# Output products of a chunked recurrence grouped by shape, and low-rank remainder products over 128 rows

## Chip, cores and metric

One core of a Trainium2 chip runs the whole forward pass in one launch. The metric is device time in microseconds (us) of an execution; smaller is better. Times before are of three runs. Clock shares say which part of full speed TensorE was granted: 1.00 is 2.4 GHz, 0.50 is 1.2 GHz.

## What is computed

A two-layer backbone over 256 latent tokens and 256 context tokens of width 1024. Each layer is a half-step SwiGLU, a token mixer, and another half-step SwiGLU. The mixer of the first layer is RWKV-7 time mixing in two directions (12 heads of 64) beside a Fourier mixing; that of the second is a gated convolution beside pooling. The change touches only the RWKV-7 part. Cut to what matters:

```python
g = jax.nn.sigmoid(gd) @ g_up
for d in range(2):
    w = jnp.exp(-DECAY_SCALE * jax.nn.sigmoid(w0[d] + jnp.tanh(wd) @ w_up[d]))   # decay, rank 64
    a = jax.nn.sigmoid(a0[d] + ad @ a_up[d])                                     # rate, rank 64
    kd = k * (1 + (a - 1) * k_a)

def step(S, inp):
    rt, wt, kt, vt, kkt, bt = inp
    sk = jnp.einsum('bhij,bhj->bhi', S, kkt)
    S = S * wt[:, :, None, :] - sk[..., None] * bt[:, :, None, :] + vt[..., None] * kt[:, :, None, :]
    return S, jnp.einsum('bhij,bhj->bhi', S, rt)

S_c, yc = wkv_scan(S0, context...)       # context first
_, yl = wkv_scan(S_c, latent...)         # then the latent tokens, whose outputs are kept
```

## The kernel before

Channels lie on partitions, tokens along the free dimension. Weights stream from HBM one 128-column tile at a time (512 KB, four buffers `wraw`) and are split into two parts, so that most products are three matmuls (`mm3`, lines 195 to 197).

The recurrence runs in chunks of 64 tokens. The 12 heads are 6 pairs; three groups of two pairs go one after the other through `chain` (line 704), each with four streams x: two pairs of heads times two directions. A chunk step does, for all four x and both heads hd: products of masked scores and state with the values (line 782, result `RH` copied by ScalarE), products with the inverse `F` (line 791, result negated into `UV` by ScalarE and VectorE), the update of the state (line 802, added into the next `XV` by VectorE, line 809), and `prep` of the next chunk (transposes 730 and 763, masked products 741 or 744, VectorE's `AG`, `RR` and `rs`, lines 748 to 759). Steps 0 to 3 are context; steps 4 to 7 are latent and also make outputs, lines 813 to 830. That is four output blocks in each of three groups, twelve in all.

An output block makes 8 sums (4 x, 2 heads), each of two products into the same PSUM columns: line 821 has `UV` against `RR`, over 128 rows; line 823 has `Xs` against `r` (`ar` for one head, `rs` for the other), over rows 0 to 63 alone. In the code they stand in turn:

```python
mm(p3[o:o + CW, x, :], lhsT=UV[:, x, hd, :], rhs=rv(S["RR"][:, hd, x, :]),
   start=True, stop=False, tile_position=(0, o), skip_group_check=True)
mm(p3[o:o + CW, x, :], lhsT=Xs[lo, x, hd, :], rhs=rv(r),
   start=False, stop=True, tile_position=(0, o), skip_group_check=True)
```

`RR`, `rs` and `Xs` have one buffer each: VectorE may write the next `RR` (line 757) and `rs` (759), and GpSimd the next `Xs` (774), only when the block has read the old ones. Each float32 product is two instruction pairs (weight load and matmul) in the trace.

Products of two ranks of 64 feed the decay and the rate. In `features` (line 541) lines 574 and 576 run over 128 rows, with the upper part of the input twice on the rows and both parts of the weight; lines 575 and 577 multiply the remainder of the input (`wa_l`, rows 0 to 63 for the decay and 64 to 127 for the rate) by the upper part of the weight, over 64 rows. There are 6 pairs of heads times 2 directions, so 24 remainder products of 512 columns. `decay_in` (line 521) makes the inputs once.

Around this, a scheduler sets the order of each engine's queue from the order of emission: while `chain` runs, `features` and `inverse` of the next group (`inverse`, line 632, is a substitution of 30 steps on VectorE) and the second layer's modulation (`ada_wide`, line 248, products of 512 columns with loads on SyncE's queue) are woven in; beside the last group stand the output projection (`project_most`, line 894) and the Fourier mixing. Each engine works its queue in order.

Of the kernel before, what the change touches and what calls it, by code (L numbers as in the profile page):

```python
# [7 lines left out]
F32 = mybir.dt.float32  # L8
F32R = mybir.dt.float32r
# [38 lines left out]
def dft():  # L48
    """[bd(cos64) | bd(sin64)] / 128, then cos256 and -sin256 by tiles of rows."""
# [13 lines left out]
def pool_counts():  # L63
    """1 / tokens of the centred windows, by the widths of the four groups."""
    t = np.arange(T)
    z = np.zeros((P, 2, T), np.float32)
    for g, w in enumerate((2, 4, 8, 16)):
        n = np.minimum(t + w - 1 - w // 2, T - 1) - np.maximum(t - w // 2, 0) + 1
        z[g % 2 * CW:g % 2 * CW + CW, g // 2, :] = 1.0 / n
    return z  # L70
# [9 lines left out]
def lay_out(a):  # L80
    """Arrays of the launch: inputs re-laid so that every load is contiguous per partition."""
# [52 lines left out]
class Net:  # L134
# [76 lines left out]
    def ada_first(self, b, r, ab):  # L211
        """Shift and scale of channel tile b of the first norm, for both streams, into columns b of ab."""
# [20 lines left out]
    def ada_rows(self, pool, vecs):  # L233
        """silu(c) along the free dimension of every partition."""
# [13 lines left out]
    def ada_wide(self, b, pool):  # L248
        """Columns 512 b .. of the second layer's modulation, in pieces of four loads."""
# [23 lines left out]
    def ada_job(self, blk, vecs):  # L273
        """Columns blk and blk + 1 of the first layer's modulation, as sums along the free dimension."""
# [13 lines left out]
    def modcol(self, l, v, m, scale=None, g=None):  # L288
        """Columns [P, KT] of modulation m; optionally scaled, or (1 + m) * g."""
# [15 lines left out]
    def stat(self, acc, hk, v, k):  # L305
        """Squares of channel tile k of stream v, added up over the tiles but the last."""
# [33 lines left out]
    def rstd_of(self, s, m, dim, eps):  # L340
        """(sum / dim + eps)^-1/2 of m blocks of tokens, a column each, to every partition."""
# [21 lines left out]
    def modulate_tile(self, k, h, vs, r, ab, yh, yl, hp):  # L363
        """y = rmsnorm(h) * a + b of channel tile k, as two float32r parts (or whole, without yl); ab[v] = (a, b) of
        stream v; r has the rates of the streams vs."""
# [14 lines left out]
    def update(self, h, k, ps, gate, acc, last=True, vs=None):  # L380
        """h += gate * ps for channel tile k of the streams vs."""
# [9 lines left out]
    def ffn(self, w, h, yh, yl, gate, acc, hp, jobs, pre, rate=None):  # L391
        """The input is normalised and shifted already; or, with rate, it is h * a with b as a column more,
        and the products get the tokens' rates of the norm."""
# [3 lines left out]
        # the first products follow the norm channel tile by channel tile  # L397
# [52 lines left out]
    def down(self, w, h, gate, acc, parts, last, jobs):  # L450
# [13 lines left out]
        # the last channel tiles stream by stream: the norm of the one during the products of the other  # L464
# [44 lines left out]
    def shift(self, m, ps, z):  # L509
        """token_shift of channel tile m from ps into z, streams side by side."""  # L510
# [10 lines left out]
    def decay_in(self, z, pool):  # L521
        """Inputs of the decay and rate projections: their upper parts in both halves of the rows, and the rest."""
        nc = self.nc
        nc.scalar.activation(z[0:CW], z[0:CW], AF.Tanh)
        w, a, l = (pool.tile([P, 2 * T], F32R, name=n) for n in ("wa_w", "wa_a", "wa_l"))
        for t, own, other in ((w, slice(0, CW), slice(CW, P)), (a, slice(CW, P), slice(0, CW))):
# [3 lines left out]
        return w, a, l  # L530
# [10 lines left out]
    def features(self, G, j, wa, kz, vz, rz):  # L541
# [9 lines left out]
        # kk: normalised per head  # L551
# [17 lines left out]
        for d in range(2):  # L569
# [5 lines left out]
            nc.tensor.matmul(pw, lhsT=uw[0:CW, d, :], rhs=wa[2][0:CW], start=False, stop=True)  # L575
            nc.tensor.matmul(pa, lhsT=ua[:, d, :], rhs=wa[1], start=True, stop=False)
            nc.tensor.matmul(pa, lhsT=ua[CW:P, d, :], rhs=wa[2][CW:P], start=False, stop=True)
# [5 lines left out]
            # log decay of a token is -DECAY / 2 * (1 + th); prefix sums per chunk  # L583
# [776 lines left out]
```

## Time and profile before

| what | us |
|---|---|
| median of 3 runs | 1640.65 |
| lowest and highest run | 1637.95, 1649.41 |
| span of the profiled execution | 1651.6 |
| TensorE matmul busy in it | 1555.6 (94%) |
| VectorE busy | 1082.6 (66%) |
| ScalarE busy | 677.3 (41%) |
| GpSimd busy | 204.9 (12%) |

The profiled execution has no time of its own beside its span. The span, from its first to its last instruction, is 10.95 us above the median of the runs, so differences worked out from the trace are taken off both. A busy TensorE is not one at its peak: ends of matmuls are modelled, and a waiting matmul counts as busy, so spacing is read from starts.

### The profile page before, as it was taken

Reading aid. Unit: us, or ns where it says so; the run is one execution under the profiler, and the core shown is the slowest. Engines: PE = TensorE matmul, PEld = TensorE weight load, DVE = VectorE, ACT = ScalarE, POOL = GpSimd, SP = SyncE. Lnnn points to the kernel's source line nnn. Section 1 sums busy time; section 2 is a strip of 40 time slices with the busy share of each in tenths; the row PEclk is TensorE's granted clock in tenths of the full one; section 3 lists DMA queues with packets and bytes.
Section 4 is the critical chain, followed back from the end, with each engine's and each line's share of the span. In section 5 each row is a group of like instructions: output and inputs, shape, how many; then the busy total and the mean of one; then the engine's idle time right before and its main releaser. Section 6 shows DMA issues by size and latency. Waiting matters only on the chain.

```text
span 1651.6 us, 29927 instructions
## 1 busy us (share of the span) xinstructions
PE 1555.6 (94%) x12102; PEld 1319.8 (80%) x12102; DVE 1082.6 (66%) x1994; ACT 677.3 (41%) x1101; POOL 204.9 (12%) x291
## 2 busy tenths in 40 slices
PE   5999999999989899899999899999999996899997
PEld 3788888888867655555587699999999985799997
DVE  4899954335689686466462577656776479767754
ACT  4431222223553542441441455444454355445442
POOL 0000100000040430330210100000000056300000
PEclk9999999999989789789995899999999997799999
DMA  9667943223222124444530355565556532435562
GB/s 370 230 242 257 346 136 103 95 84 123 77 65 96 56 93 151 158 170 148 191 104 14 116 180 186 175 187 179 181 182 176 167 102 89 141 130 185 181 177 95
DMA packets 68810, 253.40 MB, mean 153 GB/s; under 512 B 8032, under 2 KB 10864, under 8 KB 63936
## 3 DMA queue, kind: packets, MB, share of 16 engines
q1 hardware_dynamic: 64080, 219.46, 40.2%
q0 software_dynamic: 4592, 32.03, 5.4%
q8 instruction: 95, 1.56, 0.4%
q14 instruction: 43, 0.35, 0.1%
HBM read 249.36 MB, written 2.10 MB: 152 GB/s over the span
## 4 chain that ended last, share of the span: by engine, by line
PE 81%; DVE 13%; ACT 3%; issue 2%; POOL 1%; DMA 1%; SPq 0%; POOLq 0%; DVEq 0%; ACTq 0%
PE gu L195 13%; PE gu L196 13%; PE gu L197 13%; PE down L197 7%; PE down L195 7%; PE down L196 7%; PE ada L260 3%; PE mx L823 2%; PE mx L821 2%; DVE wlo L191 2%; DVE ocv L1022 1%; DVE oo L1022 1%; PE gu L1049 1%; PE pg L744 1%; PE down L802 1%
## 5 line engine op out<-in xcount | busy, mean ns | idle before, releaser
L190 ACT CAST whi<-wraw 128x1024 fp32r<-128x1024 f32 (+1 forms) x298 | 305.1, 1028 | 524.5 <-PE gu L196 224.0
L191 DVE TENSOR_TENSOR wlo<-wraw,whi 128x1024 fp32r<-128x1024 f32 (+1 forms) x298 | 356.6, 1199 | 154.0 <-ACT whi L190 146.4
L195 PE MATMUL gu<-yh,whi 128*128 128x258 f32 (+1 forms) x1408 | 438.4, 312 | 6.4 <-ACT yh L375 4.5
L196 PE MATMUL gu<-yl,whi 128*128 128x258 f32 (+1 forms) x1408 | 437.6, 311 | 0.0
L197 PE MATMUL gu<-yh,wlo 128*128 128x258 f32 (+1 forms) x1408 | 436.5, 310 | 0.2 <-DVE wlo L191 0.2
L195 PEld LDWEIGHTS gu<-yh,whi 128*128 128x128 f32 x1408 | 265.8, 189 | 24.2 <-ACT yh L375 5.7
L197 PEld LDWEIGHTS gu<-yh,wlo 128*128 128x128 f32 x1408 | 267.4, 190 | 15.2 <-DVE wlo L191 1.1
L196 PEld LDWEIGHTS gu<-yl,whi 128*128 128x128 f32 x1408 | 267.2, 190 | 14.8 <-DVE yl L377 0.9
L196 PE MATMUL down<-hl,whi 128*128 128x256 f32 (+1 forms) x704 | 217.3, 309 | 0.0
L195 PE MATMUL down<-hh,whi 128*128 128x256 f32 (+1 forms) x704 | 217.3, 309 | 0.0
L197 PE MATMUL down<-hh,wlo 128*128 128x256 f32 (+1 forms) x704 | 217.3, 309 | 0.0
L195 PEld LDWEIGHTS down<-hh,whi 128*128 128x128 f32 x704 | 134.4, 191 | 7.4
L197 PEld LDWEIGHTS down<-hh,wlo 128*128 128x128 f32 x704 | 134.4, 191 | 7.4
L196 PEld LDWEIGHTS down<-hl,whi 128*128 128x128 f32 x704 | 134.4, 191 | 7.3
L350 POOL TENSOR_TENSOR rs<-ms,mhalf 128x2 f32<-128x2 f32 (+1 forms) x9 | 10.9, 1209 | 822.8 <-DVE ms L347 822.8
L281 DVE SCALAR_TENSOR_TENSOR adaj<-adaw,cb 128x1024 f32<-128x1024 f32 x80 | 97.8, 1223 | 4.0 <-DMA adaw<-in_adat_dram 2.8
L260 PE MATMUL ada<-wraw,ccs 128*32 128x512 f32 x288 | 75.9, 669 | 1.0 <-DVE mod L269 1.0
L384 DVE SCALAR_TENSOR_TENSOR hlat<-down,mc,hlat 128x256 f32<-128x256 f32 x46 | 22.2, 483 | 62.9 <-PE down L197 62.9
L438 DVE COPY wb<-gu 128x1 f32<-128x1 f32 x132 | 20.3, 154 | 46.4 <-PE gu L197 46.4
L360 ACT CAST hh<-hd 128x256 fp32r<-128x256 f32 (+1 forms) x88 | 40.5, 461 | 23.9 <-DVE hd L433 13.1
L964 PE MATMUL gu<-yo,wraw 128*128 128x256 f32 x192 | 45.4, 396 | 1.9 <-ACT yo L375 1.9
L1006 POOL TENSOR_TENSOR opart<-opart,opr 128x256 f32<-128x256 f32 x54 | 45.2, 837 | 5.0 <-ACT opr L1004 1.2
(339 smaller groups left out, 2419.1 us busy)
## 6 DMA issues: line engine op xcount, KB each, us to landing
wraw<-in_gu_dram SPq DMA_DIRECT2D x176, 512.0 KB, 3.3
wraw<-in_ada_dram SPq DMA_DIRECT2D x72, 512.0 KB, 4.2
adaw<-in_adat_dram POOLq DMA_DIRECT2D x28, 1024.0 KB, 5.7
wraw<-in_down_dram SPq DMA_DIRECT2D x64, 448.0 KB, 3.3
wraw<-in_down_dram SPq DMA_DIRECT2D x32, 512.0 KB, 3.5
wraw<-in_win_dram SPq DMA_DIRECT2D x22, 512.0 KB, 3.5
wraw<-in_owin_dram SPq DMA_DIRECT2D x14, 512.0 KB, 3.6
ada<-in_ada_dram SPq DMA_DIRECT2D x4, 1024.0 KB, 16.8
```

The source lines that it names most:

```text
L190: nc.scalar.copy(hi[:, :k, :], raw[:, :k, :])
L191: (eng or nc.vector).tensor_tensor(out=lo[:, :k, :], in0=raw[:, :k, :], in1=hi[:, :k, :].bitcast(F32), op=ALU.subtract)
L195: mm(ps, lhsT=wh, rhs=xh, start=start, stop=False, **k)
L196: mm(ps, lhsT=wh, rhs=xl, start=False, stop=False, **k)
L197: mm(ps, lhsT=wl, rhs=xh, start=False, stop=stop, **k)
L260: nc.tensor.matmul(ps[32 * g:32 * g + 32, :], lhsT=self.cs[:, k, :], rhs=w[:, i, :], start=k < 4, stop=k >= 4, tile_position=(0, 32 * g), ...
L281: nc.vector.scalar_tensor_tensor(out=junk, in0=w[:, i, :], scalar=1.0, in1=self.cb[v], op0=ALU.mult, op1=ALU.mult, accum_out=self.mod[0, v ...
L360: self.nc.scalar.copy(hi, x)
L821: mm(p3[o:o + CW, x, :], lhsT=UV[:, x, hd, :], rhs=rv(S["RR"][:, hd, x, :]), start=True, stop=False, tile_position=(0, o), skip_group_chec ...
L823: mm(p3[o:o + CW, x, :], lhsT=Xs[lo, x, hd, :], rhs=rv(r), start=False, stop=True, tile_position=(0, o), skip_group_check=True)
L964: nc.tensor.matmul(ps[:, :n], lhsT=w[:, k, :], rhs=y[:, k, :], start=k == 0, stop=k == KT - 1)
L1006: nc.gpsimd.tensor_tensor(out=part, in0=prev, in1=pr, op=ALU.add)
```

## The change

In the output block, the eight products over 128 rows are issued first for all x and heads, and the eight over 64 rows after them. The start mark, which stood on the first product of every sum, stands on those of x = 0 alone. The remainder of the low-rank input gets a tile of 128 rows for the decay and another for the rate; GpSimd clears the other 64 rows of each with zeros once, and the remainder products run over 128 rows against the whole weight tile. Lines of the changed kernel are 2 higher from line 531 on, and 6 higher behind the output block.

```diff
     def decay_in(self, z, pool):
         nc.scalar.activation(z[0:CW], z[0:CW], AF.Tanh)
-        w, a, l = (pool.tile([P, 2 * T], F32R, name=n) for n in ("wa_w", "wa_a", "wa_l"))
-        for t, own, other in ((w, slice(0, CW), slice(CW, P)), (a, slice(CW, P), slice(0, CW))):
+        w, a, lw, la = (pool.tile([P, 2 * T], F32R, name=n) for n in ("wa_w", "wa_a", "wa_lw", "wa_la"))
+        for t, l, own, other in ((w, lw, slice(0, CW), slice(CW, P)), (a, la, slice(CW, P), slice(0, CW))):
+            nc.gpsimd.memset(l[other].bitcast(F32), 0.0)
             nc.scalar.copy(t[own], z[own])
             nc.scalar.copy(t[other], z[own])
             nc.vector.tensor_tensor(out=l[own], in0=z[own], in1=t[own].bitcast(F32), op=ALU.subtract)
-        return w, a, l
+        return w, a, lw, la
...
             nc.tensor.matmul(pw, lhsT=uw[:, d, :], rhs=wa[0], start=True, stop=False)
-            nc.tensor.matmul(pw, lhsT=uw[0:CW, d, :], rhs=wa[2][0:CW], start=False, stop=True)
+            nc.tensor.matmul(pw, lhsT=uw[:, d, :], rhs=wa[2], start=False, stop=True)
             nc.tensor.matmul(pa, lhsT=ua[:, d, :], rhs=wa[1], start=True, stop=False)
-            nc.tensor.matmul(pa, lhsT=ua[CW:P, d, :], rhs=wa[2][CW:P], start=False, stop=True)
+            nc.tensor.matmul(pa, lhsT=ua[:, d, :], rhs=wa[3], start=False, stop=True)
...
                 p3 = ps[:, :T].rearrange("p (x i) -> p x i", x=4)
+                rv = lambda x, t: t[:, ::-1] if x % 2 else t
+
                 for x in range(4):
-                    rv = (lambda t: t[:, ::-1]) if x % 2 else (lambda t: t)
+                    for hd in range(2):
+                        o = CW * hd
+                        mm(p3[o:o + CW, x, :], lhsT=UV[:, x, hd, :], rhs=rv(x, S["RR"][:, hd, x, :]),
+                           start=x == 0, stop=False, tile_position=(0, o), skip_group_check=True)
+                for x in range(4):
                     for hd in range(2):
                         o = CW * hd
                         r = S["rs"][lo, x, :] if hd else G["ar"][lo, x, c, 1, :]
-                        mm(p3[o:o + CW, x, :], lhsT=UV[:, x, hd, :], rhs=rv(S["RR"][:, hd, x, :]),
-                           start=True, stop=False, tile_position=(0, o), skip_group_check=True)
-                        mm(p3[o:o + CW, x, :], lhsT=Xs[lo, x, hd, :], rhs=rv(r),
+                        mm(p3[o:o + CW, x, :], lhsT=Xs[lo, x, hd, :], rhs=rv(x, r),
                            start=False, stop=True, tile_position=(0, o), skip_group_check=True)
```

The scheduler moves more than these lines: TensorE's queue differs from the first low-rank product on, in shape only up to the first output block, and in order from there to the end of the recurrence; behind it the queues of all engines read as before.

TensorE's queue at the last two output blocks of the third group, before (`mx` is the bank of the block; 782 and 791 are the next step's products with scores and with the inverse):

```order
L821 MATMUL mx_8236<-RR_8150,UV_8122 64x64
L823 MATMUL mx_8236<-ar_5967,Xs_8184 64x64
L821 MATMUL mx_8236<-RR_8150,UV_8122 64x64
L823 MATMUL mx_8236<-rs_8152,Xs_8184 64x64
L782 MATMUL down_8259<-XV_8121,AG_8217 64x64 x8
L791 MATMUL down_8270<-RH_8268,A_5969 64x64 x8
L821 MATMUL mx_8281<-RR_8230,UV_8123 64x64
L823 MATMUL mx_8281<-ar_5967,Xs_8257 64x64
```

The same place now (784 and 793 are the lines 782 and 791 of before):

```order
L829 MATMUL mx_8239<-ar_5970,Xs_8187 64x64
L829 MATMUL mx_8239<-rs_8155,Xs_8187 64x64
L784 MATMUL down_8262<-XV_8124,AG_8220 64x64 x8
L793 MATMUL down_8273<-RH_8271,A_5972 64x64 x8
L823 MATMUL mx_8284<-RR_8233,UV_8126 64x64 x8
L829 MATMUL mx_8284<-ar_5970,Xs_8260 64x64
L829 MATMUL mx_8284<-rs_8235,Xs_8260 64x64
```

The products of 128 rows stand together as x8, those of 64 rows behind them; what stands ahead of and behind the block is the same.

VectorE's queue at the last step of the third group, before (`XV` is the next step's state, in two halves by head; `rs` can be written only when the block ahead has read it):

```order
L809 TENSOR_TENSOR XV_8121<-down_8208,Xs_8184 64x4x64 x2
L748 TENSOR_TENSOR AG_8217<-pg_8218,cst 64x512
L757 TENSOR_TENSOR RR_8230<-pg_8218,cst 128x512
L759 COPY rs_8232<-ar_5967 64x256
L830 TENSOR_TENSOR yy_7406<-mx_8236,yy_7406 128x64 x2
```

And now:

```order
L811 TENSOR_TENSOR XV_8124<-down_8211,Xs_8187 64x4x64
L750 TENSOR_TENSOR AG_8220<-pg_8221,cst 64x512
L759 TENSOR_TENSOR RR_8233<-pg_8221,cst 128x512
L761 COPY rs_8235<-ar_5970 64x256
L811 TENSOR_TENSOR XV_8124<-down_8211,Xs_8187 64x4x64
L836 TENSOR_TENSOR yy_7409<-mx_8239,yy_7409 128x64 x2
```

The second half of `XV` moved behind the writes of `RR` and `rs`.

## Rows read from the trace of the kernel before

**Rows 1.** page, chain that ended last: by engine, by line
```profile
PE 81%; DVE 13%; ACT 3%; issue 2%; POOL 1%; DMA 1%; SPq 0%; POOLq 0%; DVEq 0%; ACTq 0%
PE gu L195 13%; PE gu L196 13%; PE gu L197 13%; PE down L197 7%; PE down L195 7%; PE down L196 7%; PE ada L260 3%; PE mx L823 2%; PE mx L821 2%; DVE wlo L191 2%; DVE ocv L1022 1%; DVE oo L1022 1%; PE gu L1049 1%; PE pg L744 1%; PE down L802 1%
```

**Rows 2.** chain by line, shares of 611:662, 720:800 and 869:914 us
```profile
by line: PE ada L260 22.5%; PE mx L823 16.6%; PE mx L821 16.3%; PE down L782 5.8%; DVE A L671 3.9%; DVE Dt L676 3.6%; PE ada L268 3.6%; PE down L791 3.6%; PE pg L744 3.3%; PE pg L741 3.2%; PE down L802 2.9%; PE mx L730 2.3%; ACT XV L732 2.3
...
by line: PE ada L260 22.4%; PE mx L823 10.3%; PE mx L821 9.9%; PE pg L744 7.2%; PE down L802 5.4%; PE ada L268 4.5%; PE misc L648 4.2%; PE down L782 4.0%; PE down L791 3.7%; ACT A L674 2.6%; PE mx L763 2.4%; ACT R L689 2.3%; ACT adas L265 2
...
by line: PE mx L821 27.1%; PE mx L823 26.8%; PE pg L744 14.1%; PE down L791 7.2%; PE down L782 7.0%; PE down L802 6.4%; PE mx L763 2.3%; PE mx L730 2.3%; PE misc L841 1.8%; ACT BK L765 1.3%; ACT UV L793 0.9%; ACT RH L785 0.8%; DVE yy L830 0
```

**Rows 3.** timeline, output block at full clock: start us, us, engine, line
```profile
633.57 0.33 PE L821 MATMUL mx<-RR,UV 128*64 128x64 f32 x2
...
633.83 0.33 PE L823 MATMUL mx<-ar,Xs 64*64 64x64 f32 x2
...
634.08 0.33 PE L821 MATMUL mx<-RR,UV 128*64 128x64 f32 x2
```

**Rows 4.** timeline, grouped run and output block at half clock
```profile
889.72 1.12 PE L782 MATMUL down<-XV,AG 128*64 128x64 f32 x16
...
890.77 0.79 PE L744 MATMUL pg<-ar,bk 64*128 64x128 f32 x2
...
897.01 0.47 PE L821 MATMUL mx<-RR,UV 128*64 128x64 f32 x2
...
903.46 1.12 PE L782 MATMUL down<-XV,AG 128*64 128x64 f32 x16
```

**Rows 5.** timeline, grouped runs at full clock, each with its follower
```profile
619.94 0.68 PE L802 MATMUL down<-UV,BK 128*64 128x64 f32 x14
620.54 0.94 PE L744 MATMUL pg<-ar,bk 64*128 64x128 f32 x12
...
641.59 0.68 PE L741 MATMUL pg<-ac,bk 64*64 64x64 f32 x16
...
642.20 1.04 PE L260 MATMUL ada<-wraw,ccs 128*32 128x512 f32 x2
```

**Rows 6.** stretches: length, busy us (instructions), clock, DMA share, GB/s
```profile
611.00:662.00 51.00, 50.12 (x476) 29.71 (x476) 34.30 (x91) 12.78 (x31) 4.82 (x9) 0.93 0.41 138
720.00:800.00 80.00, 74.69 (x978) 45.98 (x976) 49.44 (x126) 23.34 (x50) 12.19 (x18) 0.91 0.49 173
869.00:914.00 45.00, 42.87 (x303) 32.13 (x302) 11.95 (x26) 6.09 (x19) 3.16 (x3) 0.54 0.03 10
```

**Rows 7.** waits in 600:660 us: total us, times, longest
```profile
DVE RR L757 <- PE mx L821: 5.8, 3, 2.0
...
DVE yy L830 <- PE mx L823: 4.7, 1, 4.7
```

**Rows 8.** timeline of VectorE about a late output block
```profile
890.15 0.98 DVE L759 COPY rs<-ar 64x256 f32<-64x256 f32 x1
...
896.03 0.85 DVE L809 TENSOR_TENSOR XV<-down,Xs 64x256 f32<-64x256 f32 x2 [2.54 <-PE down L802]
```

**Rows 9.** timeline, 512-column and low-rank products; chain by line, 430:500
```profile
454.34 0.39 PE L196 MATMUL pg<-yl,whi 128*128 128x512 f32 x1
454.57 0.39 PE L197 MATMUL pg<-yh,wlo 128*128 128x512 f32 x1
...
685.20 0.47 PE L574 MATMUL misc<-wa_w,uw 128*128 128x512 f32 x1
...
686.88 1.91 PE L260 MATMUL ada<-wraw,ccs 128*32 128x512 f32 x12
...
by line: DVE wlo L191 11.3%; issue 9.9%; POOL inv L560 5.8%; PE pg L195 4.5%; PE pg L197 3.5%; DVE z L518 3.4%; DVE z L517 3.3%; PE misc L575 3.3%; DVE ff L589 3.3%; PE misc L574 3.3%; PE pg L196 3.2%; PE misc L629 3.1%; PE mx L197 3.0%; PE
```

**Rows 10.** timeline of GpSimd at the low-rank inputs
```profile
436.54 0.10 POOL L514 MEMSET zp<- 128x4 f32 x1 [24.05 <-DVE f L517]
```

**Rows 11.** page, DMA issues: count, KB each, median us to landing
```profile
wraw<-in_ada_dram SPq DMA_DIRECT2D x72, 512.0 KB, 4.2
```

## Prediction

> **What bounds the kernel now.** I read the chain that ended last first, since it says which engine's time is the kernel's. TensorE holds 81% of it and VectorE 13% [rows 1]; most of TensorE's part is feed-forward products, which the change leaves alone. But lines 821 and 823, a few hundred small products, stand there with about 2% each. Next I asked the chain by stretch, to see where. The twelve output blocks lie in 611 to 662 us (four, group 1), 720 to 800 us (four, group 2) and 869 to 914 us (four, group 3), and there the two lines hold 32.9%, 20.2% and 53.9% of the chain [rows 2]. That is 0.329 x 51 = 16.8 us, 0.202 x 80 = 16.2 us and 0.539 x 45 = 24.3 us, in all 57.3 us: the blocks are on the path from end to end, since TensorE works its queue in order and other engines wait behind it.
>
> Third, the timeline within a block. A row of two instructions is one product. At full clock a product starts 0.26 us after the one ahead of it, whichever of the two shapes it has [rows 3], so sixteen take 4.1 us; at half clock a block goes from 897.01 to 903.46, 6.45 us [rows 4]. The same amount of work in one shape costs far less: fourteen instructions of line 802, in the shape of line 821 (128 rows to 64 columns), are followed after 0.60 us, and sixteen of line 741, in the shape of 823 (64 rows), after 0.61 us, their followers in yet another shape [rows 5]. At half clock sixteen of line 782 take 1.05 us [rows 4]. So it isn't the products that cost, it is each turn from one row count to the other.
>
> **The change, part by part.** *Output blocks.* 32 instructions per block stay; the turns inside fall from fifteen to one. Two runs of sixteen at about 0.65 us (0.60 for fourteen, 0.61 for sixteen) make 1.3 us at full clock, two at 1.05 make 2.1 us at half clock. Groups 1 and 2: 16.8 + 16.2 = 33.0 us, less 8 x 1.3 = 10.4 us, leaves 22.6 us to win. Group 3: its first block begins at full clock, the others lie where the stretch averages 0.54 [rows 6], so 24.3 - (1.3 + 3 x 2.1) = 16.7 us.
>
> How much of that reaches the end depends on what is late next. In group 1's stretch TensorE's remaining work is 50.1 - 16.8 + 5.2 = 38.5 us, and VectorE is busy 34.3 of 51 us with the inverse of the next group woven in [rows 6]. VectorE won't stand in the way of all of it, because it waited 5.8 + 4.7 = 10.5 us for these very blocks [rows 7], and those waits go. But two engines that take turns at 38.5 and 34.3 us of work don't finish in 38.5. Group 2 is looser: VectorE has 49.4 of 80 us. I take three quarters of 22.6, that is 17.0 us; the bounds are all of it, and half (11.3 us).
>
> In group 3 no fill work is left and VectorE is busy 12 of 45 us, so nearly all counts. One new wait comes out of the queue: at the last step VectorE writes the second half of `XV` behind `RR` and `rs`, and `rs` must wait until the block has been read. Behind that `XV` TensorE's line 784 waits, and the whole rest of the step with it. Before, `XV` came first, while the block still ran. The price is a copy of `rs` at 0.98 us and half of the pair of `XV` at 0.85, so 1.4 us [rows 8]; at the least 0 if the copy is quick. 16.7 - 1.4 = 15.3 us; bounds 14 and 16.7.
>
> *Low-rank products.* Products of 512 columns that all have 128 rows follow each other every 0.23 us [rows 9]. Lines 574 to 577, where 128 and 64 rows take turns, take 686.88 - 685.20 = 1.68 us for four, 0.42 each. Four of one shape would be 0.92 us, so up to 0.76 us goes per four; there are 24 remainders, twelve fours, 9.1 us. More rows cost nothing extra here, as each product still streams 512 columns. These stand in the stretches of `features`, which alternate between engines; lines 574 and 575 are on that chain with 3.3% each, behind VectorE and GpSimd [rows 9]. I take half, 4.5 us, the middle of the bounds 0 and 9.
>
> *Zeros.* Two clears of 64x512 on GpSimd come once, where it has been idle for 24.05 us [rows 10]. They need nothing but their tiles. I cost them at nothing; if they got ahead of a clear of `zp` that is waited for, they would cost a microsecond or so, an estimate. The start marks take no time.
>
> The sum is 17.0 + 15.3 + 4.5 = 36.8 us. The profiled span goes from 1651.6 to 1614.8, and the median from 1640.65 to about 1604.
>
> One rule of the Trainium skill speaks against this. "TensorE: Matmul & The Clock Gate", part 3 on row and column tiling ("The mechanism"), says that a weight load overlaps with matmuls in flight only where it goes to another group of rows. In a run of one shape every load goes to the same rows, so by the rule grouping would put loads and products in line and gain little. The runs of line 802 [rows 5] don't show it; it is the second rival.
>
> **The rivals.**
> 1. *The weave takes it.* In groups 1 and 2 the inverse on VectorE, or loads for the fill, end as late as now, and only group 3 gains: 15.3 + 2 for some low-rank products, about 1623 us. For it: VectorE's 34.3 us, and at 652 us and later the inverse is what group 2 waits for (the transposes `A` and `Dt` are 7.5% of the chain in [rows 2]). Against it: the 10.5 us of waits in [rows 7], which end sooner. Chance 0.07.
> 2. *The change doesn't do what it says.* The 0.13 us per instruction belong to the weight loads, which stay in line in a run over the same rows. Then blocks cost what they cost now and only the low-rank part is left: 1636 us. Against it are [rows 5], runs of the same shapes at 0.04 us an instruction. Chance 0.02.
> 3. *The clock.* Shorter blocks leave TensorE waiting more often, and the stretches of groups 1 and 2, at 0.93 and 0.91 now, run like that of group 3, at 0.54 [rows 6]. If half of the 33.3 us and 58.5 us of other TensorE work there (50.1 - 16.8, 74.7 - 16.2) ran at half clock, it would take up to 46 us more; with half of that hidden among waits, 23 us go back, 1627 us. For it: group 3. Against: both stretches have fill products of 512 columns (line 260 is 22% of the chain there [rows 2]), group 3 has none left at its end. Chance 0.05.
> 4. *Slower: the fill gets ahead of the recurrence.* The scheduler has rewritten the queue from the first block on, and where it puts fill products of line 260 ahead of a step's products, in-order TensorE makes the step wait for their loads. One load lands 4.2 us after its issue [rows 11]. Were each of the sixteen steps of groups 1 and 2 to wait for one, 67 us would come on top of the forecast, 1671 us; from nine steps on (37 / 4.2) the gain is gone. Against it: DMA is busy 0.41 and 0.49 of these stretches [rows 6], and shortening them by a fifth leaves room. Chance 0.03.
>
> **How the numbers follow.** The forecast has what is left, 0.83: 1604 us. Its own range goes from all bounds at their best (22.6 + 16.7 + 9 = 48 us, 1592) to all at their worst (11.3 + 14 + 0 = 25 us, 1615). Medians of three runs that spread over 11 us add some on either side. To leave out no more than 2 in 10, I stretch it to 1588 below and over part of the first rival to 1622 above. A measurement of this kernel can tell about 1% from no change, that is 16 us, a bound at 1624. The forecast lies below it, rival 1 just about on it: faster takes 0.83 and half of rival 1, 0.87; same takes the other half, rivals 2 and 3, 0.10; slower is rival 4, 0.03.
>
> **What would show it.** Right: a block (lines 823 and 829) of 1.2 to 1.4 us at full clock and about 2.1 at half, products in it starting every 0.04 us per instruction or 0.07; the two lines' part of the chain down from 57 us to 12 to 16; the stretch from the first block of group 3 to its end down from 44 to about 28 us; VectorE's waits for `RR` shrunk; four low-rank products in about 1 us; in the last step of group 3, line 784 waiting for `XV`. Everything behind the recurrence as before. Wrong: products of a run that still start 0.13 us apart (rival 2); short blocks, but line 784 idle behind VectorE in groups 1 and 2, so that the recurrence ends no earlier there (rival 1); a granted clock well under 0.9 there (rival 3); line 260 waiting for DMA (rival 4).

## The result, and the profile after

| | median us | lowest, highest |
|---|---|---|
| before, runs beside it | 1639.3 | 1637.69, 1649.41 |
| changed | 1601.74 | 1593.66, 1603.13 |

The ratio is 0.9752, 95% interval 0.9717 to 0.9787: some 2.5% faster. The median lies 2.3 us from the forecast of 1604. In a second set of runs of the same kernel it was 1598.37 (below), so it is known to some 3 us.

I read the timeline of an output block first, as the argument rested on it. This is one of group 1, from its first products to those that follow it; it answers to [rows 3].

```profile
614.63 0.69 PE L823 MATMUL mx<-RR,UV 128*64 128x64 f32 x16
615.25 0.27 PE L829 MATMUL mx<-ar,Xs 64*64 64x64 f32 x1
...
615.86 0.69 PE L784 MATMUL down<-XV,AG 128*64 128x64 f32 x16
```

The run of 128 rows takes 0.62 us, and 1.23 us after the block's first start the next products start (615.86). Before it was 4.1 us. The block at 847.88, in group 3, takes 1.23 us too (to 849.11, below). Not every block is so short: four of the eight in groups 1 and 2 take 2.2 to 5.8 us, since TensorE's queue has products of lines 260 and 268 among theirs.

The chain by line over the three stretches with blocks now, answering to [rows 2]:

```profile
by line: PE ada L260 26.0%; PE pg L746 11.0%; PE mx L823 9.7%; PE mx L829 9.1%; PE down L804 8.6%; PE down L784 6.6%; DVE sub L666 5.7%; PE down L793 5.4%; PE ada L268 4.6%; DVE Z L668 3.2%; DVE yy L836 2.4%; ACT adas L265 2.2%; PE mx L765 
...
by line: PE ada L260 36.7%; PE pg L746 10.9%; PE mx L829 9.4%; PE mx L823 7.4%; PE ada L268 6.0%; PE down L784 5.6%; PE down L804 5.5%; ACT adas L265 5.4%; PE down L793 4.5%; PE pg L743 3.4%; PE mx L732 1.8%; PE mx L765 1.8%; issue 1.0%; DV
...
by line: DMA wraw<-in_gu_dram 10.9%; PE pg L746 9.5%; PE down L784 7.1%; PE misc L631 6.9%; PE down L793 6.2%; PE mx L829 6.0%; PE mx L823 5.9%; PE down L804 5.7%; PE misc L847 5.6%; DVE XV L811 5.5%; PE misc L854 5.2%; DVE AG L750 4.6%; is
```

Lines 823 and 829 hold 18.8% of 27 us, 16.8% of 33 and 11.9% of 31: 5.1 + 5.5 + 3.7 = 14.3 us, where the prediction gave 12 to 16 for the 57.3 of before. (In the second profiles, below, the same sums are 15.1 and 54.9 us.)

The same stretches by engine (columns of [rows 6]: length, busy us of PE, PEld, DVE, ACT, POOL, clock, DMA share, GB/s), and those between and behind:

```profile
604.00:631.00 27.00, 26.02 (x382) 16.93 (x384) 24.89 (x70) 7.94 (x22) 3.84 (x5) 1.00 0.53 195
717.00:750.00 33.00, 32.57 (x398) 18.68 (x396) 25.84 (x73) 7.86 (x23) 3.86 (x5) 1.00 0.48 173
750.00:835.00 85.00, 79.33 (x876) 58.96 (x873) 43.52 (x88) 37.24 (x65) 16.79 (x20) 0.88 0.42 139
835.00:854.00 19.00, 16.55 (x291) 13.29 (x291) 11.03 (x22) 5.98 (x19) 3.15 (x3) 1.00 0.05 16
```

Three things stand here. Groups 1 and 2 now run at a clock of 1.00, against 0.93 and 0.91 in [rows 6]. Group 3's blocks take 19 us instead of the 44 to 45, where the prediction said about 28; their clock is 1.00, where it was 0.54. And the stretch from group 2's last block to group 3's first, 750 to 835 us, has a clock of 0.88, which the prediction doesn't speak of.

VectorE's waits for the block, 10.5 us in [rows 7], are gone from group 1: between 604 and 631 us the longest wait of VectorE is one of 0.4 us.

The low-rank products, answering to [rows 9], and the wait that the prediction added, in the last step of group 3 (all engines):

```profile
576.40 0.50 PE L576 MATMUL misc<-wa_w,uw 128*128 128x512 f32 x1
...
577.20 0.40 PE L579 MATMUL misc<-wa_la,ua 128*128 128x512 f32 x1
577.53 0.33 PE L784 MATMUL down<-XV,AG 128*64 128x64 f32 x2
```

```profile
847.88 0.69 PE L823 MATMUL mx<-RR,UV 128*64 128x64 f32 x16
...
848.82 0.69 DVE L759 TENSOR_TENSOR RR<-pg,cst 128x512 f32<-128x512 f32 x1
...
849.11 0.33 PE L784 MATMUL down<-XV,AG 128*64 128x64 f32 x2
...
849.83 0.43 DVE L811 TENSOR_TENSOR XV<-down,Xs 64x256 f32<-64x256 f32 x1
...
850.31 0.68 PE L784 MATMUL down<-XV,AG 128*64 128x64 f32 x14 [0.87 <-DVE XV L811]
```

Four low-rank products take 1.13 us (576.40 to 577.53), against 1.68. And `XV` is written behind `RR` and `rs`, so that line 784 waits 0.87 us for its second half: the wait is there, at 0.87 where 1.4 was priced. The copy was the error in it. By line, the twelve copies of `rs` in the changed kernel (shortest, median, longest, in ns):

```profile
L761 DVE COPY rs<-ar x12: 288/290/1191, 545.3 to 849.5; 64x256 f32<-64x256 f32 x12
```

The median is 290 ns, here and before. The 0.98 us of [rows 8] was a copy that ran beside GpSimd's `Xs` (889.92 to 890.97 in that trace); the one at 849.53 runs alone. All copies of 0.98 to 1.19 us in the two traces, three before and two now, ran beside an `Xs`.

The page's chain by engine, answering to [rows 1]:

```profile
PE 80%; DVE 13%; ACT 2%; issue 2%; POOL 1%; DMA 1%; SPq 0%; POOLq 0%; DVEq 0%; ACTq 0%
```

It stands as it was, but the two lines are no longer among those that the page names below it.

### The profile page after: what moved, and what is told of

Its sections match the earlier page's. It is cut to its first block, busy times and chain, and to the rows that moved or that the text cites. A ratio compares the mean times of both kernels' runs of the same rounds, so it can differ in the third digit from the quotient of the medians.

```text
span 1592.0 us, 29925 instructions
## 1 busy us (share of the span) xinstructions
PE 1488.8 (94%) x12102; PEld 1279.8 (80%) x12102; DVE 1082.7 (68%) x1994; ACT 675.4 (42%) x1101; POOL 202.3 (13%) x293
## 4 chain that ended last, share of the span: by engine, by line
PE 80%; DVE 13%; ACT 2%; issue 2%; POOL 1%; DMA 1%; SPq 0%; POOLq 0%; DVEq 0%; ACTq 0%
PE gu L195 13%; PE gu L196 13%; PE gu L197 13%; PE down L195 7%; PE down L196 7%; PE down L197 7%; PE ada L260 3%; PE gu L970 1%; PE gu L1055 1%; DVE wlo L191 1%; DVE oo L1028 1%; DVE ocv L1028 1%; PE pg L746 1%; PE down L804 1%; PE misc L631 1%
## 5 line engine op out<-in xcount | busy, mean ns | idle before, releaser
L196 PEld LDWEIGHTS gu<-yl,whi 128*128 128x128 f32 x1408 | 267.2, 190 | 15.1 <-DVE yl L377 1.0
L260 PE MATMUL ada<-wraw,ccs 128*32 128x512 f32 x288 | 71.5, 625 | 0.7 <-DVE mod L269 0.7
## 6 DMA issues: line engine op xcount, KB each, us to landing
ada<-in_ada_dram SPq DMA_DIRECT2D x4, 1024.0 KB, 16.8
```

The source lines that it names most:

```text
L196: mm(ps, lhsT=wh, rhs=xl, start=False, stop=False, **k)
L260: nc.tensor.matmul(ps[32 * g:32 * g + 32, :], lhsT=self.cs[:, k, :], rhs=w[:, i, :], start=k < 4, stop=k >= 4, tile_position=(0, 32 * g), ...
```

## Experiments

All times are medians. Each kernel was compared with runs of the kernel before on the same chip, whose medians were 1639.7 to 1641.1 us in these experiments; where two kernels are set against each other it is by these, and by the length of the stretches in their profiles. I call "stretches" the pieces cut at the first and the last output product of each group.

### Second profiles of both kernels

The profiled execution of before was one of its longer ones (span 1651.6 against a median of 1640.65), that of the changed kernel its shortest (1592.0). Their difference, 59.6 us, is no measure of the change. So both were profiled once more, unchanged. (No edit.)

> The kernel before unchanged, for a second profile. Theory: the clock falls in group 3's blocks again (mean granted clock 0.45 to 0.7 there), blocks of 4.1 us at full clock in groups 1 and 2, and a span of 1630 to 1642 us, nearer to the median than the first profile's 1651.6. Rival (the fall of the clock in group 3 is the accident of one execution): a clock over 0.9 there.

> The changed kernel unchanged, for a second profile. Theory: group 3's blocks again at a granted clock of 0.9 to 1.0, the stretch between group 2's and group 3's blocks again 83 to 86 us against 77 to 79 with the old order, profiled span about 1600 us; if the 59 us between the two profiled spans was partly the luck of two executions, this one is 1597 to 1603 us. Rival (the changed kernel is really 1592 us and the other executions were disturbed): a span of 1590 to 1594 us again.

Measured: spans of 1637.1 and 1597.7 us, a difference of 39.4; the changed kernel's median in these runs was 1598.37 us (1588.94 to 1603.24), ratio 0.9727 [0.9683, 0.9771]. Group 1's blocks, group 2's, the way from there to group 3, and group 3's, before first:

```profile
606.00:645.00 39.00, 38.69 (x358) 23.95 (x356) 23.34 (x59) 7.74 (x22) 3.92 (x5) 0.91 0.34 122
...
736.00:781.00 45.00, 42.81 (x394) 25.43 (x392) 29.90 (x73) 7.81 (x22) 4.08 (x5) 0.92 0.42 140
781.00:858.00 77.00, 73.13 (x891) 54.67 (x890) 40.44 (x87) 37.12 (x65) 16.91 (x20) 1.00 0.44 146
858.00:896.00 38.00, 35.94 (x296) 26.90 (x295) 11.18 (x22) 6.08 (x19) 3.15 (x3) 0.67 0.02 8
```

```profile
607.00:633.00 26.00, 25.02 (x360) 16.10 (x358) 24.11 (x67) 7.93 (x22) 3.85 (x5) 1.00 0.55 196
...
722.00:754.00 32.00, 31.59 (x374) 17.89 (x372) 25.39 (x70) 7.84 (x22) 3.86 (x5) 1.00 0.49 172
754.00:837.00 83.00, 76.75 (x894) 58.09 (x894) 43.81 (x89) 37.24 (x65) 16.84 (x20) 0.92 0.44 142
837.00:858.00 21.00, 18.16 (x302) 14.66 (x300) 11.39 (x25) 5.99 (x19) 3.16 (x3) 0.94 0.06 23
```

Cut at the products' own starts these are 39.6, 45.0, 77.5 and 38.4 us before and 26.5, 32.3, 83.0 and 20.1 now; the way from group 1 to group 2, not shown, is 90.3 and 88.8. So 13.1 + 12.7 + 18.3 + 1.5 us are won and 5.5 us given back on the way to group 3; what lies ahead of the blocks and behind takes another 0.6 us back. The clock of group 3's blocks is 0.67 before and 0.94 now, so its fall was no accident of one execution. The low clock between group 2 and group 3 came again.

The 5.5 us are read from the timelines. First VectorE and TensorE of the changed kernel:

```profile
748.51 0.33 PE L823 MATMUL mx<-RR,UV 128*64 128x64 f32 x2
748.77 1.04 PE L260 MATMUL ada<-wraw,ccs 128*32 128x512 f32 x2
...
754.55 0.23 DVE L836 TENSOR_TENSOR yy<-mx,yy 128x64 f32<-128x64 f32 x1 [3.52 <-PE mx L829]
...
755.15 1.93 DVE L673 STREAM_TRANSPOSE A<-Z 128x1024 f32<-128x1024 f32 x1
756.94 1.95 DVE L678 STREAM_TRANSPOSE Dt<-Z 128x1024 f32<-128x1024 f32 x1
...
754.90 1.06 PE L260 MATMUL ada<-wraw,ccs 128*32 128x512 f32 x8
758.95 3.04 PE L687 MATMUL misc<-Dt,A 32*32 32x32 f32 x128 [2.99 <-DVE yy L836]
...
762.96 3.62 PE L698 MATMUL misc<-A,R 32*32 32x32 f32 x128
```

and of the kernel before:

```profile
777.61 1.97 DVE L676 STREAM_TRANSPOSE Dt<-Z 128x1024 f32<-128x1024 f32 x1
...
783.33 2.21 PE L685 MATMUL misc<-Dt,A 32*32 32x32 f32 x128
...
787.04 2.23 PE L696 MATMUL misc<-A,R 32*32 32x32 f32 x128
```

Line 836 adds the finished block into `yy`. It now stands in VectorE's queue ahead of the last steps of the next group's inverse (lines 666 and 668) and of the transposes `A` and `Dt`. It waits 3.52 us for group 2's last block. That block takes not 1.23 but 5.8 us (748.51 to 754.34), as four products of line 260 stand among its own, each about 1 us (the first at 748.77). The inverse behind `yy` waits too, and TensorE, once it has worked off what fill is left, waits 2.99 us for `Dt`. (The row names `yy`, the instruction that ended the wait by the profile; what line 687 reads is `Dt`, done at 758.89.) After that the clock is low: the 128 products of line 698 take 3.62 us instead of 2.23. Before, `Dt` was over (777.61 + 1.97 = 779.58) before TensorE needed it, and line 685, the 687 of now, starts without a wait. This is read from the traces; a kernel with `yy` put back alone, or with the fill kept out of that block, was not run, so it is argued and not shown.

### Each part alone

The outputs grouped, the low-rank products as before (against the changed kernel):

```diff
-            nc.tensor.matmul(pw, lhsT=uw[:, d, :], rhs=wa[2], start=False, stop=True)
+            nc.tensor.matmul(pw, lhsT=uw[0:CW, d, :], rhs=wa[2][0:CW], start=False, stop=True)
...
-            nc.tensor.matmul(pa, lhsT=ua[:, d, :], rhs=wa[3], start=False, stop=True)
+            nc.tensor.matmul(pa, lhsT=ua[CW:P, d, :], rhs=wa[2][CW:P], start=False, stop=True)
```

> The changed kernel with the low-rank products as before (remainders over 64 rows); only the output blocks are grouped. Theory (turns between row counts cost, in both places): the blocks' part stays, the low-rank part of 4.5 us (bounds 0 and 9) is missing, so 1601.7 + 4.5 = about 1606 us, 1602 to 1611. Rival (the gain comes from the low-rank part, which is ahead on the path, and the weave takes that of the blocks): 1625 us or more.

and the other way round, the low-rank products over 128 rows and the block product by product:

```diff
-                rv = lambda x, t: t[:, ::-1] if x % 2 else t
...
-                           start=x == 0, stop=False, tile_position=(0, o), skip_group_check=True)
                 for x in range(4):
...
+                        mm(p3[o:o + CW, x, :], lhsT=UV[:, x, hd, :], rhs=rv(S["RR"][:, hd, x, :]),
+                           start=True, stop=False, tile_position=(0, o), skip_group_check=True)
```

> The kernel before with only the low-rank remainders over 128 rows; the output blocks take turns as before. Theory: blocks of 4.1 us at full and 6.45 us at half clock as before, four low-rank products in about 1.0 to 1.2 us, 1639.3 - 4.5 = about 1635 us, 1630 to 1639. Rival (the weave hides the low-rank part): no change, 1639 us.

Measured: 1603.31 us, ratio 0.9774 [0.9727, 0.982], with the outputs alone; 1639.12 us, ratio 0.9985 [0.9959, 1.0011], with the low-rank products alone. The low-rank part is worth 1.6 us by the first (1603.31 - 1601.74) and 2.5 by the second (0.0015 x 1640); neither can be told from nothing. For the second 1635 us had been expected; it came out where the rival had it. The products themselves are quicker, 1.13 us for four against 1.68, so most of that time seems not to have been on the path: they stand where VectorE and GpSimd end last [rows 9].

### Which groups pay

The old turns in group 3 alone, and in groups 1 and 2 alone (`if G["g"] < 2` in its place); against the changed kernel:

```diff
+                if G["g"] == 2:
+                    for x in range(4):
+                        rv = (lambda t: t[:, ::-1]) if x % 2 else (lambda t: t)
+                        for hd in range(2):
...
+                            mm(p3[o:o + CW, x, :], lhsT=UV[:, x, hd, :], rhs=rv(S["RR"][:, hd, x, :]),
+                               start=True, stop=False, tile_position=(0, o), skip_group_check=True)
+                            mm(p3[o:o + CW, x, :], lhsT=Xs[lo, x, hd, :], rhs=rv(r),
+                               start=False, stop=True, tile_position=(0, o), skip_group_check=True)
+                else:
```

> The changed kernel with the output products of the third group alone in the order of before. Forecast's term for group 3: 15.3 us, so 1601.7 + 15.3 = 1617 us. Theory now (taking turns for some 3 us also lets the granted clock fall, and everything between the last blocks then runs at half clock): clock near 1.0 up to the third group's first block, falling in it, from there to the end of the last block about 40 us instead of 19, so 1601.7 + 20 = about 1622 us, 1616 to 1628. Rival (the clock falls anyway when the fill ends, in other executions of the changed kernel too): tail at half clock in the changed kernel's other executions as well, so only 4 x 2.9 to 4 x 4.3 = 12 to 17 us, 1614 to 1619 us.

> The changed kernel with the output products of groups 1 and 2 in the order of before, the third grouped. Theory: the forecast's three quarters of 22.6 us, 17 us, so 1619 us, 1612 to 1625; the granted clock dips at the end of blocks in groups 1 and 2 and stays up in group 3. Rival (the weave takes the gain of these groups: what ends earlier there is waited for later): 1602 to 1607 us.

Measured: 1618.79 us (ratio 0.986 [0.9819, 0.9902]) and 1621.88 us (0.988 [0.9841, 0.992]). So grouping is worth 17.1 us in group 3 and 20.1 us in groups 1 and 2; with 2 us for the low-rank products that is 39, the whole of the gain. These go by the changed kernel's 1601.74; by its second median, 1598.37, each of the two is 3.4 us larger. And 1618.79 us lies in the range of the theory for group 3 as well as in its rival's: the clock decides between them, not the time. Group 3's stretch with its turns back, and the stretches from group 2 to group 3 and of group 3 with the turns back in groups 1 and 2:

```profile
839.00:878.00 39.00, 37.25 (x296) 28.08 (x294) 11.13 (x23) 6.08 (x19) 3.15 (x3) 0.64 0.02 6
```

```profile
781.00:859.00 78.00, 74.11 (x914) 55.45 (x912) 40.73 (x88) 37.14 (x65) 16.93 (x20) 1.00 0.45 147
859.00:879.00 20.00, 17.70 (x290) 14.28 (x286) 10.75 (x22) 5.99 (x19) 3.16 (x3) 0.90 0.02 5
```

Two things can be read here. With the old order in group 2 the way to group 3 is 77.5 us at a clock of 1.00, as before the change: the 5.5 us go with the grouping of these groups, which fits the timelines. And the clock of group 3 hangs on its own turns: 0.64 with them, 0.90 and more without, in the same places of the same program. (Without them it can fall too, but only in the last block, which in this kernel and in the second profile of the changed one takes 2.3 us from its first start to its last, and 1.5 in the first profile.) The timeline of its second block in the kernel with its turns back shows the fall:

```profile
849.88 0.33 PE L824 MATMUL mx<-RR,UV 128*64 128x64 f32 x2 [0.68 <-ACT BK L767]
850.14 0.33 PE L826 MATMUL mx<-ar,Xs 64*64 64x64 f32 x2
...
853.22 0.47 PE L826 MATMUL mx<-ar,Xs 64*64 64x64 f32 x2
853.62 0.47 PE L824 MATMUL mx<-RR,UV 128*64 128x64 f32 x2
...
861.71 0.47 PE L824 MATMUL mx<-RR,UV 128*64 128x64 f32 x2
...
868.17 1.12 PE L784 MATMUL down<-XV,AG 128*64 128x64 f32 x16
```

Up to 853.22 a product starts 0.26 us after the other and lasts 0.33 for two instructions; from there 0.40 and 0.47, and the third block takes 6.46 us (861.71 to 868.17). From the start of this block (849.88, after a wait of 0.68 us) TensorE has no gap in its row when this sets in; it is going through turns.

### How many turns

Runs of two products (7 turns inside a block in place of 1; against the changed kernel):

```diff
-                           start=x == 0, stop=False, tile_position=(0, o), skip_group_check=True)
-                for x in range(4):
+                           start=True, stop=False, tile_position=(0, o), skip_group_check=True)
```

> The changed kernel with the output products grouped only within each x: two over 128 rows, then two over 64 rows, so seven turns inside a block instead of one, or fifteen before. Theory (a turn costs (4.1 - 1.23) / 14 = 0.205 us at full clock): blocks of 1.23 + 6 x 0.205 = 2.5 us, twelve blocks 15 us longer than in the changed kernel, of which three quarters reach the end: about 1613 us, 1608 to 1619. Rival (a product waits for the one ahead in the same sum): none follows its own sum directly here, so blocks as in the changed kernel and 1602 us.

And no turns, though in the order of before: all products over 128 rows, `Xs` and `rs` with zeros on the upper rows (against the block of the kernel before; the low-rank products stay as changed):

```diff
-                        r = S["rs"][lo, x, :] if hd else G["ar"][lo, x, c, 1, :]
+                        r = S["rs"][:, x, :] if hd else G["ar"][:, x, c, 1, :]
...
-                        mm(p3[o:o + CW, x, :], lhsT=Xs[lo, x, hd, :], rhs=rv(r),
+                        mm(p3[o:o + CW, x, :], lhsT=Xs[:, x, hd, :], rhs=rv(r),
```

> The changed kernel with the output products back in the order of before, taking turns within each sum, but all over 128 rows: the second product gets zeros in the other 64 rows of Xs (written once per group) and the full rows of r. Theory (only the row count that turns costs, not the order): blocks of about 1.2 to 1.4 us as in the changed kernel, 1600 us, 1594 to 1606. Rival (a product that adds to the sum of the one just ahead has to wait for it, and grouping took that away): blocks of 4 us and more, about 1635 us.

In that kernel one tile `rs` serves all steps and a block reads the `rs` of the step behind it, so its outputs are not those of the reference and only its time counts. The next one gives each step its own again, its upper rows cleared by GpSimd at every step:

```diff
                 rs = S["rs"] = t([P, 4, CW], "rs", 1)
+                nc.gpsimd.memset(rs[up], 0.0)
...
+        Xs = t([P, 4, 2, CW], "Xs", 1)
+        nc.gpsimd.memset(Xs[up], 0.0)
```

> As the run before with products in turn over 128 rows, whose block read the rs of the step behind; here rs is one tile per step again, its other 64 rows cleared each time by GpSimd. Theory (only a change of the row count costs): blocks of about 1.0 us, 32 instructions at 0.03 us and no turn, 1594 to 1602 us. Rival (the order within a sum costs): blocks of 4 us, 1635 us.

Measured: runs of two 1604.56 us (0.9783 [0.9736, 0.983]); one shape 1596.06 (0.9729 [0.9674, 0.9784]) and, with each step's `rs`, 1593.21 (0.9696 [0.965, 0.9743]). A block of group 3 with runs of two, and one of the last kernel:

```profile
845.67 0.34 PE L822 MATMUL mx<-RR,UV 128*64 128x64 f32 x4
...
846.20 0.34 PE L822 MATMUL mx<-RR,UV 128*64 128x64 f32 x4
...
847.78 0.69 PE L784 MATMUL down<-XV,AG 128*64 128x64 f32 x16
```

```profile
836.10 0.34 PE L825 MATMUL mx<-RR,UV 128*64 128x64 f32 x4
...
837.08 0.68 PE L786 MATMUL down<-XV,AG 128*64 128x64 f32 x16
```

The block of runs of two takes 2.11 us, that of one shape 0.98 although its products alternate as they did before. So within a block neither the order nor what is added where costs anything; the shape does. From the block of one shape a turn can be priced (turns inside the block, and the one at its end): (4.10 - 0.98) / 16 = 0.195 us before, (2.11 - 0.98) / 8 = 0.14, (1.23 - 0.98) / 2 = 0.13 in the changed kernel. "TensorEngine Tiling (Array Packing)" of the Trainium skill, "Key Properties", says that a change of the tiling mode, other than one of the tile, drains TensorE. The traces agree with a cost at such a change, though not what TensorE does in it: from 128 to 64 rows each turn costs 0.13 to 0.2 us at full clock, while the two heads, which go to different columns in turn, cost nothing.

For runs of two 1613 us had been expected, 1608 to 1619, with blocks of 2.5 us; both came out lower. By these blocks twelve would be 12 x 0.88 = 10.6 us longer than the changed kernel's, an estimate, and the time is only 2.8 us longer (6.2 by the second median). Its way from group 2 to group 3 is 79.9 us against 83.0, and the list of TensorE's waits has none for `Dt` there, so what the changed kernel gives back is in part kept here. And its clock stays at 1.00 in group 3. Half the turns (7 for 15) cost about a third: 1.13 us a block over the 0.98, for 3.12.

### No copy at all

The second head's `Xs` can stand on the upper rows, where `ar` of that head already lies; then `rs` isn't needed, and every product has 128 rows. Grouped as in the changed kernel:

```diff
-                rs = S["rs"] = t([P, 4, CW], "rs", 1)
-                nc.vector.tensor_copy(rs[lo], G["ar"][up, :, c, 1, :])
...
+                    nc.gpsimd.tensor_tensor(out=Xs[CW * hd:CW * hd + CW, :, hd, :], in0=XV[lo, :, hd, :],
...
-                        r = S["rs"][lo, x, :] if hd else G["ar"][lo, x, c, 1, :]
-                        mm(p3[o:o + CW, x, :], lhsT=Xs[lo, x, hd, :], rhs=rv(x, r),
+                        mm(p3[o:o + CW, x, :], lhsT=Xs[:, x, hd, :], rhs=rv(x, G["ar"][:, x, c, 1, :]),
```

> A version meant to beat the changed kernel: grouped as there, but Xs of the second head is written to rows 64 to 127 and the other rows of Xs stay zero, so that the second product of both heads runs over 128 rows against ar itself. No turn is left in a block, the copy rs and its waits are gone (12 copies of 0.3 to 1.2 us on VectorE), GpSimd makes Xs in two pieces. Theory: blocks of 1.0 us, the late step's wait for rs gone, 1592 to 1600 us. Rival (blocks are no longer what is late, weave and latency are): 1600 to 1604 us as the changed kernel.

and the same with the products in the order of before:

```diff
-                           start=x == 0, stop=False, tile_position=(0, o), skip_group_check=True)
-                for x in range(4):
-                    for hd in range(2):
-                        o = CW * hd
+                           start=True, stop=False, tile_position=(0, o), skip_group_check=True)
                         mm(p3[o:o + CW, x, :], lhsT=Xs[:, x, hd, :], rhs=rv(G["ar"][:, x, c, 1, :]),
```

> Every product of an output block has 128 rows (head 2 takes the state it needs from the upper rows, no copy rs), and the order is the old one, product by product in turn. Theory (the turn of row counts is the whole cost, and the order is free): a block of 16 takes 0.98 us as in the other interleaved kernel of one shape, the granted clock in group 3's blocks stays at 1.0, and the time is 1590 to 1599 us. Rival (the interleaved order itself costs something, each product accumulating in another column range than the one before): blocks over 1.5 us, clock in group 3 under 0.8, time over 1610 us.

Measured: 1599.47 us (0.9746 [0.9697, 0.9795]) grouped, and 1590.54 us (0.969 [0.9656, 0.9724], 1589.17 to 1593.23) in turn. The last step of group 3 in the latter:

```profile
844.69 0.88 DVE L811 TENSOR_TENSOR XV<-down,Xs 64x256 f32<-64x256 f32 x2 [1.14 <-PE down L804]
...
845.15 0.34 PE L822 MATMUL mx<-RR,UV 128*64 128x64 f32 x4
...
845.60 0.69 DVE L750 TENSOR_TENSOR AG<-pg,cst 64x512 f32<-64x512 f32 x1
...
846.35 0.69 PE L784 MATMUL down<-XV,AG 128*64 128x64 f32 x16
```

Both halves of `XV` are written together again, ahead of `AG`, from 844.69 to 845.57. The block starts at 845.15 and would be over at 846.13 by its 0.98 us; line 784 starts at 846.35, when `AG` (845.60 + 0.69 = 846.29) is there, so of the 0.87 us some 0.2 are left. This is the best of the kernels: 11.2 us under the changed kernel's first median, 7.8 under its second (1598.37). The two kernels without `rs` do the same products and differ by 8.9 us; TensorE's wait at line 687 behind group 2 is 2.7 us in the grouped one and 2.1 in the other, and group 2's blocks take 32.3 and 29.5 us. Behind group 2 both still have the wait for `Dt`, and line 698 takes 3.62 us in both. That accounts for a part of the 8.9 us; the rest I did not take apart.

### The wait for `XV`

```diff
-                rs = S["rs"] = t([P, 4, CW], "rs", 1)
+                rs = S["rs"] = t([P, 4, CW], "rs", 2)
```

> The changed kernel with two buffers for rs, so that the copy of a step does not wait for the products of the step before. Theory (the products that wait for XV in the last step of a group cost under 1 us each time, three times in the program): the 0.87 us wait of the 14 products for XV in the last step stays under 0.5 us, and the time stays at 1598 to 1604 us. Rival (rs is what paces the steps of the chain, 24 times): 1590 us or less.

Measured: 1603.5 us (0.9759 [0.9718, 0.98]), no gain. The wait:

```profile
857.02 0.69 DVE L759 TENSOR_TENSOR RR<-pg,cst 128x512 f32<-128x512 f32 x1
...
857.73 0.43 DVE L811 TENSOR_TENSOR XV<-down,Xs 64x256 f32<-64x256 f32 x1
...
858.21 0.68 PE L784 MATMUL down<-XV,AG 128*64 128x64 f32 x14 [0.57 <-DVE XV L811]
```

`rs` no longer stands between `RR` and `XV`, but `RR` does, and 0.57 us of the 0.87 stay, a little over what was expected. The wait is a matter of VectorE's queue, more than of the buffer.

## Why the prediction was right

**What bounds.** The twelve blocks were on the path from end to end: the two lines held 57.3 us of the chain and now hold 14.3; of the 43 us between, 5.5 were given back, and the medians differ by 37.6 (1639.3 - 1601.74). That 43 less 5.5 comes so near to this is chance, as the second profiles give 39.8 for the 43. That it is the turn and not the product is shown by the blocks of one shape (0.98 us in the old order). Rival 2 is out with that. The rule that a load overlaps only with products on other rows (the Trainium skill, "TensorE: Matmul & The Clock Gate", part 3, "The mechanism", which also names a load into the background weight buffer) does not set the pace of these runs: sixteen instructions over the same rows start within 0.62 us.

**Groups 1 and 2**: 17.0 us forecast, bounds 11.3 and 22.6; 20.1 measured. The size was near, the place of the loss was not. I took a quarter off because VectorE's 34.3 us beside TensorE's 38.5 would hold up the stretch itself. They didn't: the blocks' stretches shrank by 13.1 + 12.7 us, more than the 22.6 of the sum, with the clock up from 0.91 and 0.92 to 1.00. What was lost was lost behind group 2, where, by the timelines, `yy` ahead of the inverse makes TensorE wait 3.0 us, after which the clock is low. That is rival 1's mechanism (the inverse ends late) with rival 3's (a lower clock) behind it, at 5.5 us between them in place of 19 and 23, and in a stretch that neither named. I had read the order of VectorE's queue in the last step of group 3 only.

**Group 3**: 15.3 us forecast, bounds 14 and 16.7; 17.1 measured, 18.3 in the second profiles. The term that was mis-sized is the block at half clock: three of four were put at 2.1 us, because the stretch averages 0.54 [rows 6]. I took this clock for a property of the stretch. It belongs to the turns: without them the clock is 0.90 to 1.00, three of the four blocks are 1.2 to 1.3 us, and the other products of the stretch run faster too: it takes 19 to 20 us where about 28 was foretold. That the gain did not come out larger still is because before, too, the clock differs between executions (0.54 in the first profile [rows 6], 0.67 in the second), and the sum was made from the slower one: its stretch took 43.7 us, that of the second 38.4. The two errors cancelled, and that is luck. The new wait was foreseen, at 0.87 us for 1.4, the copy of `rs` being mis-sized.

**Low-rank products**: 4.5 us forecast; about 2 measured, inside the bounds 0 and 9. Four of them take 1.13 us where 0.92 was priced, so by this one four TensorE saves 12 x 0.55 = 6.6 us, an estimate, of which some third shows in the time. I took half of 9.

**Zeros**: nothing, and nothing was seen; the two clears took 0.52 us each, at 422.62 and 423.19, and no engine's wait names them.

**The sum**: 20.1 + 17.1 + 2 = 39.2 us measured by parts, 36.8 forecast. That the total came within 2.3 us owes something to luck: groups 1 and 2 and group 3 were put too low by 3.1 and 1.8 us, the low-rank products too high by 2.5. Rival 4 did not come: the list of TensorE's waits between 604 and 835 us names no load.

## What to carry to other kernels

Where small products of two row counts stand in turn, price the turn by comparing starts within a run of one shape with starts across the change; on this path each cost 0.13 to 0.2 us, more than the product itself. The turn can go by order or by filling the shorter operand with zeros, and the second needs no new order of the products. Here the kernels that filled the rows and kept the old order were the fastest, 1590.54 to 1596.06 us; filled and grouped, it was 1599.47, no better than the changed kernel. The wait behind group 2 stayed in all of them, at 1.7 to 2.7 us. After grouping, look in every queue at what now waits for the end of the whole group, and what stands behind it.

## What was not expected of the hardware

The granted clock fell inside a block without gaps in TensorE's row (849.88 to 853.22), in stretches where row counts take turns: 0.64 in group 3 with its turns back, 0.90 to 1.00 without, and 1.00 with half as many. In the profile such a stretch reads as 96% busy (37.25 of 39 us). So a busy share near all does not say that the clock holds. Which property of the turns lets it fall, the runs don't say.
